# The MLP's first product as seven products of quarter operands, with weight sums partly by accumulating DMAs

## The chip, the cores and the metric
The kernel runs on one core of a Trainium2 chip. The metric is the time of one execution on the device in microseconds; the median of three runs is shown with the lowest and the highest.

## The reference
One layer of a diffusion backbone on 512 tokens of 1024 features, in float32. A token mixer of three branches (retention, Fourier, spatial gating) comes first; the part that matters here is the second sub-layer:

```
h2 = modulate(rms_norm(x, g_pre_mlp[l]), sh2, sc2)
x = x + gt2 * rms_norm(sq_relu_mlp(h2, w_up[l], w_down[l]), g_post_mlp[l])

def sq_relu_mlp(h, w_up, w_down):
    a = jax.nn.relu(h @ w_up)
    return (a * a) @ w_down
```
`w_up` is 1024 x 4096, `w_down` 4096 x 1024.

## The kernel before
Activations lie transposed, features on partitions and tokens on the free axis. Each float32 operand is written once in two parts of the type float32r, `hi` (the rounded part, written by ACT, L105 or L126) and `lo` (the exact rest, by DVE, L108 or L127). A product of 128 features by 128 features on some tokens is three instructions on PE, hi*hi, hi*lo and lo*hi, accumulated in PSUM (`mm3`, L131 to L133).

PE and SP (the queue of the weight loads) keep the order in which the program is written; the instructions of the other engines are ordered when the program is built, by priority and readiness, and each engine then runs its list in that order. Weights come in chunks of 128 x 1024 values (512 KB), in the order of `plan`: `fetch` loads one into `raw` (3 buffers, L102) and splits it into `whi` and `wlo` (3 buffers each). `chunk(kind, n, ahead)` hands one out and fetches the next ones. `slots` are 28 buffers of 4 KB a partition for long-lived tiles, `aux` 9 of the same size. `background` (L387) loads one row block of `w_mod` on POOL's queue into a tile `wmod2` (2 buffers), once PE's latest product is done, and runs the matvec of the one before on DVE (L240).

Before the MLP the output projection runs in two halves of 256 tokens (`out_proj`), and the norm of one half (`mix_residual`, then `mlp_input`) behind the products of the other. Both begin with `total` (L851), a sum over partitions by PE; the reciprocal root (`rstd`) and the rest are on DVE and ACT. `mlp_input` writes the MLP's input h2 in two parts, one feature tile at a time (L248, L252, L253). The first quarter of the hidden features (`up_first`, L935) is taken in the two halves of 256 tokens, for each row tile of `w_up` that meets an h2 tile; the three further quarters (`up`) are products of 512 tokens. `activate` takes relu and square on ACT and splits the hidden features. `down` follows a quarter behind and adds into y on DVE (L980); the last quarter's `down` runs in halves again (`last_down`, L1003), and `finish` adds the residual and stores. The order of the products around the first quarter is:

```
    up_first(0, 0)
    up_first(0, 1)
    mix_residual(1)
    for k in range(2, 7):
        up_first(0, k)
    mlp_input(1)
    up_first(0, 7)
    up_first_done(0)
```
Of the kernel before, what the change touches and what calls it, by code (L numbers as in the profile page):

```python
# [16 lines left out]
F32 = mybir.dt.float32  # L17
# [18 lines left out]
def kernel(ctx: ExitStack, tc: tile.TileContext, i: dict, out: bass.AP):  # L36
# [42 lines left out]
    plan += [("upr", k) for k in range(KT)] + [("up", KT + m) for m in range(KT)]  # L79
    for q in range(1, 4):  # L80
        plan += [("down", KT * (q - 1) + m) for m in range(KT)]
        plan += [("up", KT * (q + 1) + m) for m in range(KT)] if q < 3 else []
    plan += [("down", 24 + m) for m in range(KT)]
# [3 lines left out]
    place.update({("upr", k): aux if 2 <= k <= 5 else slot for k in range(KT)})  # L87
    place.update({("down", 24 + m): slot for m in range(6)})
    source = {"kq": "w_kq", "u": "w_u", "vs": "w_vs", "f": "w_f", "gate": "w_gate", "v": "w_v", "dft_l": "dft_l",
              "k": "w_k", "g": "w_g", "out": "w_out", "abc": "w_abc", "upr": "w_up0", "up": "w_up", "down": "w_down"}  # L90
# [4 lines left out]
    def fetch(later=False):  # L95
        """Load the next [128, 1024] weight chunk of the plan and split it into (hi, lo)."""
# [5 lines left out]
        nc.sync.dma_start(out=raw, in_=i[source[key[0]]][{"v": key[1] % 4, "up": key[1] - KT}.get(key[0], key[1])])  # L102
# [15 lines left out]
    def chunk(kind, n, ahead=2):  # L118
        """A chunk of weights in two parts; the next ones of the plan are on their way."""
# [9 lines left out]
    def mm3(ps, w, x, first, last):  # L129
        """ps += w.T @ x with w = (hi, lo), x = (hi, lo)."""  # L130
# [7 lines left out]
    def product(ps, w, xs_, sl=slice(None)):  # L138
        """ps = w.T @ x for a chunk w of 8 row tiles."""
        for k in range(KT):  # L140
            ks = slice(128 * k, 128 * k + 128)
            mm3(ps, (w[0][:, ks], w[1][:, ks]), hl(xs_[k], sl), k == 0, k == KT - 1)

# [30 lines left out]
    vecs = const.tile([P, 10, KT], F32, name="vecs")       # b_mod (6), g_pre_mix, g_post_mix, g_pre_mlp, g_post_mlp  # L174
# [10 lines left out]
    def keep_warm(n):  # L185
        """Products that nobody reads, so that the tensor engine's clock is up when the data are there."""
# [23 lines left out]
    def rstd(sums, n, size, r, between=None):  # L210
        """r = (sum / n + eps) ** -0.5: a table's estimate and one Newton step. The sums are in PSUM, side by side."""
# [923 lines left out]
```

## Time and profile before

| | us |
|---|---|
| median of 3 runs (lowest to highest) | 794.76 (794.74 to 796.51) |
| the profiled execution, first to last instruction (span) | 793.4 |
| PE busy in it | 779.8 |
| DVE busy | 496.0 |
| ACT busy | 388.7 |

The span is the profiled execution's own time between its first and last instruction; what a run has around it is seen from the difference to the median, 1.4 us. PE's busy time is the time in which at least one product is in its pipeline, so neighbouring products overlap in it: one product is busy for longer than the distance to the next. Idle time of an engine that nobody waits for costs nothing.

### The profile page before, as it was taken

How to read it: one execution, taken by the hardware profiler on the slowest of the kernel's cores; microseconds unless marked ns; L12 is line 12 of the kernel's file. 1: busy time of each engine (PE TensorE's matmuls, PEld its weight loads, DVE VectorE, ACT ScalarE, POOL GpSimd, SP SyncE). 2: the span in 40 equal slices, each digit the busy share in tenths (PEclk: the TensorE clock that was granted, in tenths of full speed). 3: DMA queues.
4: the chain of work that ended last, by engine and by line, in shares of the span. 5: the costliest groups of instructions: out<-in, count | busy, mean ns of one | idle time of the engine just before them, and what ended most of it. 6: DMA issues, size and time to landing. Idle time of an engine off the chain costs nothing.

```text
span 793.4 us, 10284 instructions
## 1 busy us (share of the span) xinstructions
PE 779.8 (98%) x4066; PEld 668.7 (84%) x4066; DVE 496.0 (63%) x731; ACT 388.7 (49%) x585; POOL 38.1 (5%) x73
## 2 busy tenths in 40 slices
PE   9999999999999999999999999999999999999994
PEld 6888888888888888888999998888888888888993
DVE  6999997688898576599369735631333333336255
ACT  6337557657997443332477455432353124524222
POOL 0061000000000111100000001000000000000001
PEclk9999999999999999999999999999999999999997
DMA  9954242643224487635124024623223223225011
GB/s 346 379 179 133 93 138 81 204 152 108 87 99 137 154 296 264 227 116 193 49 87 141 11 81 159 205 88 107 98 88 107 92 94 107 88 98 186 1 54 54
DMA packets 31680, 106.74 MB, mean 135 GB/s; under 512 B 3704, under 2 KB 5888, under 8 KB 31632
## 3 DMA queue, kind: packets, MB, share of 16 engines
q1 hardware_dynamic: 26944, 89.25, 32.9%
q0 software_dynamic: 4672, 16.82, 6.2%
q8 instruction: 32, 0.52, 0.3%
q14 instruction: 16, 0.13, 0.1%
q10 hardware_dynamic: 16, 0.01, 0.0%
HBM read 103.97 MB, written 2.10 MB: 134 GB/s over the span
## 4 chain that ended last, share of the span: by engine, by line
PE 97%; DVE 2%; ACT 0%; issue 0%; POOL 0%; DVEq 0%; ACTq 0%; POOLq 0%
PE ps L132 27%; PE ps L133 27%; PE ps L131 27%; PE pu L935 5%; PE kq L356 5%; PE warm L189 1%; DVE y L1021 1%; PE ps L201 1%; PE ssx L273 0%; PE ps L473 0%; PE ps L472 0%; PE ps L471 0%; PE ps L649 0%; DVE sg L548 0%; PE ps L851 0%; DVE wlo L108 0%
## 5 line engine op out<-in xcount | busy, mean ns | idle before, releaser
L105 ACT ACTIVATE whi<-raw 128x1024 fp32r<-128x1024 f32 (+1 forms) x119 | 124.2, 1045 | 234.2 <-PE ps L132 201.5
L108 DVE TENSOR_TENSOR wlo<-raw,whi 128x1024 fp32r<-128x1024 f32 (+1 forms) x119 | 143.3, 1204 | 121.0 <-ACT whi L105 120.9
L133 PE MATMUL ps<-h,wlo 128*128 128x512 f32 x448 | 174.4, 389 | 0.3 <-DVE wlo L108 0.3
L131 PE MATMUL ps<-h,whi 128*128 128x512 f32 x448 | 174.7, 390 | 0.0
L132 PE MATMUL ps<-h,whi 128*128 128x512 f32 x448 | 174.4, 389 | 0.0
L133 PEld LDWEIGHTS ps<-h,wlo 128*128 128x128 f32 x448 | 84.1, 188 | 18.4 <-DVE wlo L108 0.8
L131 PEld LDWEIGHTS ps<-h,whi 128*128 128x128 f32 x448 | 84.1, 188 | 17.5
L132 PEld LDWEIGHTS ps<-h,whi 128*128 128x128 f32 x448 | 84.1, 188 | 17.1
L131 PE MATMUL ps<-a,whi 128*128 128x512 f32 (+1 forms) x224 | 83.7, 374 | 0.0
L132 PE MATMUL ps<-a,whi 128*128 128x512 f32 (+1 forms) x224 | 83.7, 374 | 0.0
L133 PE MATMUL ps<-a,wlo 128*128 128x512 f32 (+1 forms) x224 | 83.7, 374 | 0.0
L240 DVE CUSTOM_DVE_ANT_0 wmod<-wmod,cb,vecs 128x1024 f32<-128x1024 f32 x32 | 41.0, 1282 | 24.7 <-DMA wmod<-in_w_modT 24.7
L131 PEld LDWEIGHTS ps<-a,whi 128*128 128x128 f32 x224 | 42.2, 188 | 7.5
L133 PEld LDWEIGHTS ps<-a,wlo 128*128 128x128 f32 x224 | 42.2, 188 | 7.5
L132 PEld LDWEIGHTS ps<-a,whi 128*128 128x128 f32 x224 | 42.2, 188 | 7.4
L935 PE MATMUL pu<-h,rhi 128*128 128x256 f32 x256 | 45.6, 285 | 0.3 <-ACT h L252 0.3
L127 DVE TENSOR_TENSOR a<-relu,a 128x512 fp32r<-128x512 f32 (+1 forms) x40 | 22.7, 584 | 27.5 <-ACT a L126 27.5
L935 PEld LDWEIGHTS pu<-h,rhi 128*128 128x128 f32 x256 | 39.2, 192 | 0.5 <-ACT h L252 0.5
L387 POOL DMA_DIRECT2D wmod<-in_w_modT x32 | 17.0, 531 | 433.1 <-PE ps L133 230.8
L980 DVE TENSOR_TENSOR y<-y,ps 128x512 f32<-128x512 f32 x16 | 11.0, 686 | 40.9 <-PE ps L133 40.9
L935 PE MATMUL pu<-h,rlo 128*128 128x256 f32 x128 | 33.9, 283 | 0.0
L108 DVE TENSOR_TENSOR rlo<-raw,rhi 128x1024 fp32r<-128x1024 f32 x19 | 22.9, 1221 | 9.9 <-ACT rhi L105 9.1
(292 smaller groups left out, 1436.3 us busy)
## 6 DMA issues: line engine op xcount, KB each, us to landing
wmod<-in_w_modT POOLq DMA_DIRECT2D x32, 512.0 KB, 3.5
raw<-in_w_up SPq DMA_DIRECT2D x32, 512.0 KB, 3.3
raw<-in_w_down SPq DMA_DIRECT2D x32, 512.0 KB, 3.3
raw<-in_w_gate SPq DMA_DIRECT2D x24, 512.0 KB, 4.3
wmod<-in_w_modT SPq DMA_DIRECT2D x16, 512.0 KB, 8.5
x<-in_xT SPq DMA_DIRECT2D x8, 512.0 KB, 6.5
raw<-in_w_kq SPq DMA_DIRECT2D x8, 512.0 KB, 6.9
raw<-in_w_v SPq DMA_DIRECT2D x8, 512.0 KB, 4.0
```

Of the source, the lines that this page charges most:

```text
L105: S.activation(out=hi, in_=raw, func=AF.Copy)
L108: rest = lambda: V.tensor_tensor(out=lo, in0=raw, in1=f32(hi), op=ALU.subtract)
L127: V.tensor_tensor(out=dst_lo, in0=src, in1=f32(dst_hi), op=ALU.subtract)
L131: PE.matmul(ps, w[0], x[0], start=first, stop=False)
L132: PE.matmul(ps, w[0], x[1], start=False, stop=False)
L133: latest[0] = PE.matmul(ps, w[1], x[0], start=False, stop=last)
L189: PE.matmul(ps, ones, ones.unsqueeze(1).broadcast_to([P, 4, P]), start=True, stop=True)
L240: return V.tensor_tensor_reduce(out=prod, in0=wt, in1=cvec, scale=1.0, scalar=bias_col, op0=ALU.mult, op1=ALU.add, accum_out=dst_col)
L356: PE.matmul(kq[n], w[sub % 2][:, 128 * n:128 * n + 128], hs[k][:, sub // 2], start=k == 0 and sub == 0, stop=False)
L387: load = nc.gpsimd.dma_start(out=t, in_=i["w_modT"][j, k])
L935: latest[0] = PE.matmul(ps, w[a][:, 128 * m:128 * m + 128], x[b], start=k == 0 and (a, b) == parts[0] and m % 2 == 0, stop=k == KT - 1 and ...
L980: V.tensor_tensor(out=yk(m), in0=yk(m), in1=ps, op=ALU.add)
```

## The change
The up product is cut into quarters in three directions: the features of h2 in a lower and an upper half (rows 1 and 2), the tokens in two halves (N1, N2), and each pair of hidden feature tiles in its two tiles. Such a product of 2 x 2 blocks takes eight products of blocks; the changed kernel takes seven, of sums of blocks, for each of 16 units of two hidden feature tiles (`seventh`: 4 row tiles x 3 instructions of 256 tokens). On the side of the activations seven operands of four feature tiles each are kept in two parts: B11, B21, B22 and the sums T1 to T4 (`in_parts`, `mlp_sums`). On the side of the weights a unit has four operands: a (tile 2u as it is), b (two sums), c (w2 with the sum of its halves in the lower half) and d (one sum). `unit_weights` loads both tiles into two `raw` buffers (r1, r2). Three accumulating DMAs on POOL's queue (256 KB each) add parts of the weights in HBM to r2, r1 and x, and one sum is a DVE addition (x, in a `wmod2` buffer); ACT and DVE split a, b, c and d. A unit's outputs are combined from two accumulators in PSUM into a raw tile t by ACT and DVE, relu and square are one DVE instruction on t, and `split_hidden` writes the two parts.

The first products of units 0 to 7 (with a, on the first half of the tokens) run while the second half's norms are computed (`early`); the other five products of these units follow, then the down products of the first quarter, and units 8 to 11 and 12 to 15 after the first and the second quarter's. The pools keep their sizes. The diff removes the comments of the file as well, which is left out here.

```diff
-    plan += [("upr", k) for k in range(KT)] + [("up", KT + m) for m in range(KT)]
+    plan += [("upa", u) for u in range(KT)] + [("down", m) for m in range(4 * KT)]
...
-    h2 = [slot([P, 2, L], F32R, "h2") for _ in range(KT)]
+    full, parts = {}, {}
+    def in_parts(name, src, where):
+        hi, lo = where([P, 4, HT], F32R, "bhi"), where([P, 4, HT], F32R, "blo")
+        S.activation(out=hi, in_=src, func=AF.Copy)
+        V.tensor_tensor(out=lo, in0=src, in1=f32(hi), op=ALU.subtract)
+        parts[name] = (hi, lo)
     def mlp_input(half):
         r = tmp("rx2", HT)
         rstd([total(sums[half][:, 1])], D, HT, r)
...
+        for j in range(2):
+            b = full[j, half] = slot([P, 4, HT], F32, "h2")
+            for m in range(4 * j, 4 * j + 4):
+                if m % 2 == 0:
+                    pair = work.tile([P, 2, HT], F32, name="xr2", tag="t")
+                xr = pair[:, m % 2]
+                scaled(xr, xk(m)[:, halves[half]], gs2[:, m:m + 1], r)
+                S.activation(out=b[:, m % 4], in_=xr, func=AF.Identity, bias=mod[:, 3, m:m + 1])
             if half == 0:
+                in_parts(("B11", "B21")[j], b, slot)
+    def mlp_sums():
+        b11, b12, b21, b22 = full[0, 0], full[0, 1], full[1, 0], full[1, 1]
+        n2 = slot([P, 4, HT], F32, "n2")
+        V.tensor_tensor(out=b11, in0=b11, in1=b12, op=ALU.subtract)
+        V.scalar_tensor_tensor(out=n2, in0=b11, scalar=-1.0, in1=b22, op0=ALU.mult, op1=ALU.subtract)
+        in_parts("T2", n2, aux)
+        V.tensor_tensor(out=b12, in0=b22, in1=b12, op=ALU.subtract)
+        in_parts("T3", b12, aux)
+        in_parts("T1", b11, aux)
+        V.scalar_tensor_tensor(out=b21, in0=n2, scalar=-1.0, in1=b21, op0=ALU.mult, op1=ALU.subtract)
+        in_parts("T4", b21, aux)
+        in_parts("B22", b22, slot)
+    raw_hidden, hidden = {}, {}
+    weights = {}
+    def unit_weights(u):
+        w1, w2 = i["w_up"][2 * u], i["w_up"][2 * u + 1]
+        lower, upper = slice(0, 512), slice(512, 1024)
+        r1 = raw_pool.tile([P, D], F32, name="r1", tag="raw")
+        nc.sync.dma_start(out=r1, in_=w1)
+        r2 = raw_pool.tile([P, D], F32, name="r2", tag="raw")
+        nc.sync.dma_start(out=r2, in_=w2)
+        yield
+        if (u, "a") not in weights:
+            a = hi_pool.tile([P, D], F32R, name="whi", tag="whi"), lo_pool.tile([P, D], F32R, name="wlo", tag="wlo")
+            with tc.high_priority(offset=30):
+                split(*a, r1)
+            weights[u, "a"] = a
+        nc.gpsimd.dma_start(out=r2[:, lower], in_=w2[:, upper], accum_op=ALU.add)
+        yield
+        x = raw_pool.tile([P, 512], F32, name="s2", tag="wmod2", bufs=2)
+        with tc.high_priority(offset=30):
+            V.tensor_tensor(out=x, in0=r2[:, lower], in1=r1[:, lower], op=ALU.add)
+        nc.gpsimd.dma_start(out=r1[:, lower], in_=w2[:, lower], accum_op=ALU.add)
+        yield
+        b = hi_pool.tile([P, D], F32R, name="whi", tag="whi"), lo_pool.tile([P, D], F32R, name="wlo", tag="wlo")
+        with tc.high_priority(offset=30):
+            split(b[0][:, lower], b[1][:, lower], x)
+            split(b[0][:, upper], b[1][:, upper], r1[:, lower])
+        weights[u, "b"] = b
+        nc.gpsimd.dma_start(out=x, in_=w1[:, upper], accum_op=ALU.add)
+        yield
+        c = hi_pool.tile([P, D], F32R, name="whi", tag="whi"), lo_pool.tile([P, D], F32R, name="wlo", tag="wlo")
+        with tc.high_priority(offset=30):
+            split(*c, r2)
+        weights[u, "c"] = c
+        yield
+        d = hi_pool.tile([P, D], F32R, name="whi", tag="whi"), lo_pool.tile([P, D], F32R, name="wlo", tag="wlo")
+        with tc.high_priority(offset=30):
+            split(d[0][:, lower], d[1][:, lower], x)
+        weights[u, "d"] = d
+        yield
+    steps_of = {}
+    def prepare(u, n):
+        if u is None:
+            return
+        if u not in steps_of:
+            steps_of[u] = [unit_weights(u), 0]
+        while steps_of[u][1] < n:
+            next(steps_of[u][0])
+            steps_of[u][1] += 1
+    def seventh(ps, u, w, upper, x, first=False):
+        hi, lo = weights[u, w]
+        for k in range(4):
+            ks = slice(512 * upper + 128 * k, 512 * upper + 128 * k + 128)
+            for n, (a, b) in enumerate(((hi, 0), (hi, 1), (lo, 0))):
+                latest[0] = PE.matmul(ps, a[:, ks], parts[x][b][:, k], start=first and k == 0 and n == 0,
+                                      stop=k == 3 and n == 2, skip_group_check=True)
+    chain = {}
+    urgent = dict(offset=100)
+    N1, N2 = halves
+    def unit_first(u):
+        if u not in chain:
+            chain[u] = bank("chain")[:, 0:HT]
+        t = raw_hidden[u] = slot([P, 2, L], F32, "ru")
+        seventh(chain[u], u, "a", 0, "B11", True)
+        with tc.high_priority(**urgent):
+            S.copy(out=t[:, 0, N1], in_=chain[u])
+        p2 = bank()[:, 0:HT]
+        seventh(p2, u, "a", 1, "B21", True)
+        with tc.high_priority(**urgent):
+            V.tensor_tensor(out=t[:, 0, N1], in0=t[:, 0, N1], in1=p2, op=ALU.add)
+    def unit_rest(u):
+        t, ch = raw_hidden[u], chain[u]
+        following = None if u in (7, 11, 15) else u + 1
+        side = bank()[:, 0:HT]
+        prepare(following, 1)
+        seventh(ch, u, "b", 0, "T2")
+        with tc.high_priority(**urgent):
+            S.activation(out=t[:, 1, N1], in_=ch, func=AF.Copy, scale=-1.0)
+        seventh(side, u, "b", 1, "T3", True)
+        with tc.high_priority(**urgent):
+            S.activation(out=t[:, 1, N2], in_=side, func=AF.Copy, scale=-1.0)
+        prepare(following, 3)
+        seventh(ch, u, "c", 0, "T1")
+        with tc.high_priority(**urgent):
+            V.tensor_tensor(out=t[:, 1, N2], in0=t[:, 1, N2], in1=ch, op=ALU.subtract)
+        seventh(side, u, "c", 1, "T4")
+        with tc.high_priority(**urgent):
+            V.tensor_tensor(out=t[:, 1, N1], in0=t[:, 1, N1], in1=side, op=ALU.subtract)
+        prepare(following, 5)
+        seventh(ch, u, "d", 0, "B22")
+        with tc.high_priority(**urgent):
+            S.copy(out=t[:, 0, N2], in_=ch)
+        prepare(following, 6)
+        V.scalar_tensor_tensor(out=t, in0=t, scalar=0.0, in1=t, op0=ALU.max, op1=ALU.mult)
+    def split_hidden(u):
+        t = raw_hidden.pop(u)
+        hi, lo = slot([P, 2, L], F32R, "ahi"), slot([P, 2, L], F32R, "alo")
+        split(hi, lo, t)
+        for e in range(2):
+            hidden[2 * u + e] = (hi[:, e], lo[:, e])
...
+    def early(pair):
+        ps = bank("chain")
+        for u in (2 * pair, 2 * pair + 1):
+            weights[u, "a"] = chunk("upa", u, min(2, 7 - u))
+            chain[u] = ps[:, halves[u % 2]]
+            t = raw_hidden[u] = slot([P, 2, L], F32, "ru")
+            seventh(chain[u], u, "a", 0, "B11", u % 2 == 0)
+        for u in (2 * pair, 2 * pair + 1):
+            p2 = bank()[:, 0:HT]
+            seventh(p2, u, "a", 1, "B21", True)
+            t = raw_hidden[u][:, 0, N1]
+            S.copy(out=t, in_=chain[u])
+            V.tensor_tensor(out=t, in0=t, in1=p2, op=ALU.add)
+    early(0)
     mix_residual(1)
-    for k in range(2, 7):
-        up_first(0, k)
+    early(1)
     mlp_input(1)
-    up_first(0, 7)
-    up_first_done(0)
-    for k in range(KT):
-        up_first(1, k)
-        with tc.issue_after(last_lo[0].ins):
-            prefetch("up", KT + min(k // 2, 2))
-    up_first_done(1)
+    early(2)
+    early(3)
+    mlp_sums()
+    prepare(0, 6)
+    for u in range(KT):
+        unit_rest(u)
+        if u < 4:
+            split_hidden(u)
+        background()
...
-        product(ps, chunk("down", KT * q + m), [hidden[KT * q + k] for k in range(KT)])
+        product(ps, chunk("down", KT * q + m, min(2, 7 - m)), [hidden[KT * q + k] for k in range(KT)])
         if q == 0:
             S.copy(out=yk(m), in_=ps)
         else:
             V.tensor_tensor(out=yk(m), in0=yk(m), in1=ps, op=ALU.add)
-    for m in range(KT):
-        up(1, m)
-        background()
     V.tensor_tensor(out=gg2, in0=mod[:, 5], in1=vecs[:, G_POST2], op=ALU.mult)
-    for q in range(1, 4):
+    for q in range(3):
         for m in range(KT):
-            down(q - 1, m)
-        if q < 3:
-            for m in range(KT):
-                up(q + 1, m)
+            down(q, m)
+            if q < 2 and m >= 4:
+                prepare(8 + 4 * q, m - 3)
+                if m == 7:
+                    prepare(8 + 4 * q, 6)
+        for u in range(4 * q + 4, 4 * q + 8):
+            split_hidden(u)
+            if q < 2:
+                unit_first(u + 4)
+                unit_rest(u + 4)
...
-        "w_up0": _rows(a["w_up"][0][:, :D], 1),
-        "w_up": _tiles(a["w_up"][0][:, D:]),
+        "w_up": _tiles(a["w_up"][0]),
```

## Rows read from the trace of the kernel before

**Rows 1.** First part of the page: busy time, share of the span, instructions.
```profile
PE 779.8 (98%) x4066; PEld 668.7 (84%) x4066; DVE 496.0 (63%) x731; ACT 388.7 (49%) x585; POOL 38.1 (5%) x73
```
**Rows 2.** Stages by windows: PE, PEld, DVE, ACT, POOL busy (instructions), granted clock, DMA share, GB/s.
```profile
4.00:8.00 4.00, 4.00 (x14) 1.98 (x14) 2.40 (x4) 2.63 (x4) 0.24 (x1) 1.00 1.02 376
...
425.30:472.80 47.50, 47.23 (x391) 46.92 (x390) 30.34 (x60) 24.74 (x61) 0.00 (x0) 1.00 0.17 57
472.80:516.00 43.20, 43.20 (x193) 35.78 (x192) 24.77 (x35) 24.86 (x46) 3.70 (x7) 1.00 0.52 169
...
560.00:733.70 173.70, 173.70 (x768) 143.85 (x768) 66.52 (x69) 68.38 (x87) 0.00 (x0) 1.00 0.31 106
```
**Rows 3.** What PE waited for in the whole run: us in total, times, longest.
```profile
PE warm L189 <- POOL eps_h L167: 1.0, 1, 1.0
...
PE pu L935 <- ACT h L252: 0.3, 1, 0.3
```
**Rows 4.** The chain that ended last, in order of time: start, us, what.
```profile
425.48 5.76 PE pu L935 x48
431.24 0.43 PE ps L851 x2
431.67 14.39 PE pu L935 x120
446.06 0.45 PE ps L851 x2
```
**Rows 5.** Timelines of PE, DVE and ACT around the norms of both halves: start, us, instruction.
```profile
423.01 1.28 DVE L248 SCALAR_TENSOR_TENSOR xr<-x,gs,rx 128x256 f32<-128x256 f32 x3
...
425.31 0.88 PE L935 MATMUL pu<-h,rhi 128*128 128x256 f32 x6
...
434.81 2.36 DVE L887 TENSOR_TENSOR y<-y,ry 128x1024 f32<-128x1024 f32 x2
...
437.08 2.49 DVE L888 TENSOR_TENSOR x<-x,y 128x512 f32<-128x512 f32 x4
...
442.25 0.43 DVE L850 TENSOR_TENSOR sums<-sums 128x256 f32<-128x256 f32 x1
...
448.54 1.28 DVE L248 SCALAR_TENSOR_TENSOR xr<-x,gs,rx 128x256 f32<-128x256 f32 x3
...
453.81 0.91 ACT L252 ACTIVATE h<-xr,mod 128x256 fp32r<-128x256 f32 x2 [0.53 <-DVE xr L248]
```
**Rows 6.** Instructions of four tiles: ns min/median/max, first and last start.
```profile
L105 ACT ACTIVATE whi<-raw x119: 627/1061/1067, 14.3 to 732.5; 128x1024 fp32r<-128x1024 f32 x115, 128x516 fp32r<-128x516 f32 x4
L108 DVE TENSOR_TENSOR wlo<-raw,whi x119: 678/1225/1227, 16.3 to 733.5; 128x1024 fp32r<-128x1024 f32 x115, 128x516 fp32r<-128x516 f32 x4
...
L873 ACT ACTIVATE y<-ps x16: 363/383/385, 381.5 to 425.9; 128x256 f32<-128x256 f32 x16
...
L1003 DVE TENSOR_TENSOR y<-y,ps x16: 414/421/422, 737.0 to 780.6; 128x256 f32<-128x256 f32 x16
...
L240 DVE CUSTOM_DVE_ANT_0 wmod<-wmod,cb,vecs x32: 1272/1284/1289, 186.9 to 514.9; 128x1024 f32<-128x1024 f32 x32
```
**Rows 7.** Waits of SP's and POOL's queues from 380 us on: total, times, longest.
```profile
SPq L102 <- DVE wlo L108: 257.2, 48, 20.1
...
POOL wmod L387 <- PE ps L133: 29.5, 6, 4.9
```
**Rows 8.** DMA issues: KB each, median us to landing.
```profile
wmod<-in_w_modT POOLq DMA_DIRECT2D x32, 512.0 KB, 3.5
raw<-in_w_up SPq DMA_DIRECT2D x32, 512.0 KB, 3.3
...
raw<-in_w_gate SPq DMA_DIRECT2D x24, 512.0 KB, 4.3
wmod<-in_w_modT SPq DMA_DIRECT2D x16, 512.0 KB, 8.5
...
out_y<-x SPq DMA_DIRECT2D x8, 256.0 KB, 2.2
```
**Rows 9.** Landing times of the tile raw.
```profile
DMA to landing us min/median/max: 2.6/3.6/10.9
```
**Rows 10.** The end of the run by windows, columns as in rows 2.
```profile
782.00:784.00 2.00, 0.22 (x2) 0.00 (x0) 1.10 (x3) 0.90 (x3) 0.00 (x0) 1.00 0.00 0
784.00:786.00 2.00, 0.00 (x0) 0.00 (x0) 1.97 (x4) 0.00 (x0) 0.96 (x1) 0.83 0.00 0
786.00:788.00 2.00, 0.00 (x0) 0.00 (x0) 2.00 (x3) 0.00 (x0) 1.32 (x2) 0.50 0.21 74
```

More of the change, by code (lines that the diff above doesn't have):

```diff
@@ L86 @@
     place[("out", 7)] = slot
-    place.update({("upr", k): aux if 2 <= k <= 5 else slot for k in range(KT)})
     place.update({("down", 24 + m): slot for m in range(6)})
     source = {"kq": "w_kq", "u": "w_u", "vs": "w_vs", "f": "w_f", "gate": "w_gate", "v": "w_v", "dft_l": "dft_l",
-              "k": "w_k", "g": "w_g", "out": "w_out", "abc": "w_abc", "upr": "w_up0", "up": "w_up", "down": "w_down"}
+              "k": "w_k", "g": "w_g", "out": "w_out", "abc": "w_abc", "upa": "w_up", "down": "w_down"}
     ready = {}
@@ L101, in fetch @@
         raw = raw_pool.tile([P, size], F32, name="raw", tag="raw")
-        nc.sync.dma_start(out=raw, in_=i[source[key[0]]][{"v": key[1] % 4, "up": key[1] - KT}.get(key[0], key[1])])
+        nc.sync.dma_start(out=raw, in_=i[source[key[0]]][{"v": key[1] % 4, "upa": 2 * key[1]}.get(key[0], key[1])])
         hi = where([P, 1024], F32R, "rhi") if where else hi_pool.tile([P, size], F32R, name="whi", tag="whi")
@@ L141, in product @@
             ks = slice(128 * k, 128 * k + 128)
-            mm3(ps, (w[0][:, ks], w[1][:, ks]), hl(xs_[k], sl), k == 0, k == KT - 1)
+            x = xs_[k]
+            x = (x[0][:, sl], x[1][:, sl]) if isinstance(x, tuple) else hl(x, sl)
+            mm3(ps, (w[0][:, ks], w[1][:, ks]), x, k == 0, k == KT - 1)
     xs, wmod1 = [], []
@@ L893, in mlp_input @@
         rstd([total(sums[half][:, 1])], D, HT, r)
-        for m in range(KT):
-            if m % 2 == 0:
-                pair = work.tile([P, 2, HT], F32, name="xr2", tag="t")
-            xr = pair[:, m % 2]
-            scaled(xr, xk(m)[:, halves[half]], gs2[:, m:m + 1], r)
-            last_lo[0] = shifted(h2[m][:, 0, halves[half]], h2[m][:, 1, halves[half]], xr, mod[:, 3, m:m + 1])()
-    hidden = {}
-    def activate(n, sl, ps):
-        r = tmp("relu", sl.stop - sl.start)
-        S.activation(out=r, in_=ps, func=AF.Relu)
-        S.activation(out=r, in_=r, func=AF.Square)
-        split(hidden[n][:, 0, sl], hidden[n][:, 1, sl], r)
@@ L911, in up @@
-    def up(q, m):
-        n = KT * q + m
-        w = chunk("up", n)
-        hidden[n] = (aux if q % 2 else slot)([P, 2, L], F32R, "a2")
-        ps = bank()
-        product(ps, w, h2)
-        activate(n, slice(0, L), ps)
-    last_lo = [None]
-    wu = []
-    pus = {}
-    def up_first(half, k):
-        if half == 0:
-            wu.append(chunk("upr", k, min(3, 7 - k)))
-        if k == 0:
-            pus[half] = [bank("pu") for _ in range(4)]
-        w = wu[k]
-        x = hl(h2[k], halves[half])
-        parts = ((0, 0), (1, 0), (0, 1))
-        for m, (a, b) in ([(m, p) for p in parts for m in range(KT)] if k == 0 else
-                          [(m, p) for m in range(KT) for p in parts]):
-            ps = pus[half][m // 2][:, HT * (m % 2):HT * (m % 2) + HT]
-            latest[0] = PE.matmul(ps, w[a][:, 128 * m:128 * m + 128], x[b],
-                                  start=k == 0 and (a, b) == parts[0] and m % 2 == 0,
-                                  stop=k == KT - 1 and (a, b) == parts[2], skip_group_check=True)
@@ L939, in up_first_done @@
-    def up_first_done(half):
-        for m in range(KT):
-            if half == 0:
-                hidden[m] = slot([P, 2, L], F32R, "a2")
-            activate(m, halves[half], pus[half][m // 2][:, HT * (m % 2):HT * (m % 2) + HT])
+        for j in range(2):
[6 more added lines that the diff above has]
+                S.activation(out=b[:, m % 4], in_=xr, func=AF.Identity, bias=mod[:, 3, m:m + 1])
+            if half == 0:
+                in_parts(("B11", "B21")[j], b, slot)
@@ L950 @@
         out_proj(1, m)
-        prefetch("upr", min(m, 4))
     mlp_input(0)
@@ L980, in down @@
             V.tensor_tensor(out=yk(m), in0=yk(m), in1=ps, op=ALU.add)
-    for m in range(KT):
-        up(1, m)
-        background()
     V.tensor_tensor(out=gg2, in0=mod[:, 5], in1=vecs[:, G_POST2], op=ALU.mult)
-    for q in range(1, 4):
+    for q in range(3):
         for m in range(KT):
-            down(q - 1, m)
-        if q < 3:
-            for m in range(KT):
-                up(q + 1, m)
+            down(q, m)
[8 more added lines that the diff above has]
+                unit_rest(u + 4)
     wd = {}
```

5 lines of the change are left out of this document (removed).

## The prediction
> **What bounds the kernel now.** I read the page's first part, the stages by windows, the waits, the chain of waits around the start of the MLP, the DMA issues. The reader is to see that PE is busy 98% of the span at the full clock [rows 1], and in the MLP without a gap, while DVE is busy 30.3 of 47.5 us in the first quarter of the up product and 24.8 of 43.2 in the second, and ACT about as much or less [rows 2]. PE's longest wait on anything in the whole run is 1.0 us, and 0.3 in front of any product of the MLP [rows 3]. So the kernel's time is its list of products, and the change is worth what it takes off that list, less every gap that it opens, because today there are none.
>
> What a product costs is its distance to the next one, not its busy time: 48 products of 256 columns take 5.76 us and 120 take 14.39 [rows 4], 0.120 each; 768 of 512 columns take 173.7 [rows 2], 0.226 each. Two of 256 cost 0.240, 6% more than one of 512.
>
> **The change part by part.**
>
> *Products.* Before: the first quarter in 384 products of 256 (46.1 us), three quarters in 576 of 512 (130.3): 176.4 us. After: 16 units of 7 x 12 products, 1344 of 256 columns: 161.3. Minus 15.1 us; one eighth fewer columns would be 22, but the narrow ones give a third back. The down products keep number and shape.
>
> *Operands of the first half later: +2.0 (0 to 2.5).* Before, PE needs only one feature tile of h2 to begin, and waited 0.3 us for it [rows 3]. After, B11 wants four tiles, then a split over 1024 elements: `scaled` four times at 0.40 (three in 1.28 less overlap), an Identity 0.45 [rows 5], hi 1.06, lo 1.22 [rows 6]: 4.3 us from the norm's factor, which is there at 423.0. Before, the first product starts 2.3 us after that point, at 425.3 [rows 5].
>
> *Less cover between two norms: +5.2 (4.5 to 5.7).* PE's queue has the two sums over partitions (`total`) of the second half in order. Before, 120 products lie between them, 14.4 us [rows 4]. The work they cover runs from the first, 431.24, to the last sum on DVE, 442.25 + 0.43 [rows 5]: 11.4 us. After, only early(1) stands there, 48 products, 5.76 us, and the second `total` blocks PE, since early(2) and early(3) are queued behind it. 11.4 - 0.4 - 5.8 = 5.2.
>
> *The seven sums' operands: +5 (0 to 11).* From the second `total` to T2: the root 2.5 us (446.06 to 448.54), eight `scaled` 3.2, an Identity 0.5, two sums at 1.18 (two of 1024 in 2.36), hi 1.06, lo 1.2 [rows 5, 6]: 10.8; early(2) and (3) cover 96 x 0.12 = 11.5. But the same DVE has in that time a chunk's lo, the first unit's sum and splits, four additions: 4.8 more. 0 to 4 late; I take 2. T1, T3, T4 and B22 are six more DVE instructions of 1.18, 7.1 us, beside a first unit whose PE time is 60 x 0.12 = 7.2 and which has its own 7.6 of DVE (next paragraph). 0 to 7; I take 3.
>
> *The early eight units: +19.6 (3 to 34, and 104 in the worst case).* Each has 7.2 us of products. DVE's part per unit, at 0.62 for 512 elements, 1.18 for 1024, 0.42 for 256 (grouped rows [rows 5]): x 0.62, b 1.24, c 1.18, d 0.62, two evacuations 0.84, relu squared 1.18; a hidden split 1.18 in four of eight and one w_mod row 1.28 [rows 6] in all: 7.6 on average. DVE alone would be the bound, by 0.4 us a unit plus what is left of the operands above. The longer chain is in the buffers. `raw` has three, and a unit holds two (r1, r2) until its splits are done, so r2 of unit u+1 can't be loaded before a buffer of unit u is free; SP waits for just this today (DVE's lo, 257 us in 48 waits [rows 7]), at no cost because a chunk then lasts 5.4 us of PE. From there: load 3.3, accumulating DMA into r2, and then either the split of r2 (1.06 + 1.22) frees the buffer, or the sum x 0.62, the second accumulating DMA into r1, and the split of half of it (0.62 + 0.62). No row has an accumulating DMA. From below 2.2 (a 256 KB store), from above 8.5 (512 KB where all queues were full at 376 GB/s [rows 2]); I take 3.5, the loads on POOL's queue, whose path it shares [rows 8]. The short loop is 3.3 + 3.5 + 2.3 = 9.1, the long one 3.3 + 3.5 + 0.6 + 3.5 + 1.2 = 12.1. Which closes first is a matter of how ACT's and DVE's queues are written, which no row shows; r2's data are there 4.1 us earlier, so I take 9.1 and 0.9 for queueing behind a DVE that is busy three quarters of it: 10.0, so 2.8 us of PE idle at each of seven handovers. Low end: DVE's bound, 7 x 0.4; high end: the long loop, 7 x 4.9, or with two accumulations of 8.5 a loop of 22.1, 7 x 14.9. Waits also move to POOL: its queue holds the three accumulations and the w_mod load, which waits for a unit's last product; POOL waits for PE up to 4.9 us at a time today [rows 7], and an accumulation behind it would wait as long. I take nothing for it.
> [...]
>
> *The later eight: +4 (0 to 12).* 84 products, 10.1 us, against 9.1 or 12.1; six handovers, units 8 and 12 being prepared behind the down products, where DVE is idle (66.5 of 173.7 us busy [rows 2]). I take 0.7 each.
>
> *What hides.* Evacuations between the products of one accumulator: 12 others lie between, 1.44 us, against 0.38 to 0.42 [rows 6] and at worst an ACT split of 1.06 ahead: nothing (up to 0.2 each). 16.8 MB more traffic: under 250 GB/s in the densest stretch, where loads took 4.3 instead of 3.3 [rows 8]; that is in the 0.9. ACT: 5 of 7.2 us.
>
> **Sum.** -15.1 + 2.0 + 5.2 + 5 + 19.6 + 4 = +20.7 on a span of 793.4: 814.1. The median of the runs is 1.4 above the span: 815.
>
> **The rivals.**
> 1. *The list of products decides (faster).* The order of ACT and DVE lets r2 go early, the w_mod rows slip behind, and only the gap of 5.2 and the 2.0 remain: 794.8 - 15.1 + 7.2 = 787. For it: PE has hardly waited for anything so far [rows 3]. Against it: that was with splits of 2.3 us in 5.4; now DVE has more than 100%. Chance 0.11.
> 2. *DVE is the bound, not the DMAs.* The early eight cost 7.1 + 8 x 0.4 = 10, the later none: 794.8 - 15.1 + 7.2 + 2 + 10 = 799. For it: the quickest load of a chunk landed in 2.6 us [rows 9]. Chance 0.13; a hand's breadth better on one term gives no change, 0.07.
> 3. *The long loop (slower still).* r1 is freed first: 7 x 4.9 + 6 x 2.0 = 46.3 in place of 23.6: 838. It decides as soon as an accumulation takes over 4 us or b's split stands before c's. Chance 0.18.
> 4. *The clock.* [...] Chance 0.09. [...]
>
> **How the numbers follow.** The forecast has 0.42. Range 786 to 850: left out are half of rival 1 and most of rival 4; an accumulation of 8.5 us would be far outside and has no load to match it. What a measurement here can tell from no change is 0.3%, 792.4 to 797.1. Faster 0.11 (rival 1), same 0.07, slower 0.82.
>
> **What would show it.** The gap in PE before the second `total` of about 5 us; in each of units 1 to 7 a wait of PE's weight load for the lo of b (DVE), that for a DMA from w_up, and SP waiting for DVE; DVE near 80% in that stretch; products at 0.120. Wrong, if PE runs the 16 units without gaps of over a microsecond, or if the early stretch from `early(0)` to the first down product lasts less than 23 + 58 + 10 us.

## The result: 878 us in place of 795, and the profile after

The changed kernel took 877.87 us (median of four, 877.73 to 881.06), the kernel before 794.95: a ratio of 1.105 (95% interval 1.103 to 1.107). The forecast was 815, its range 786 to 850: the sign held, the size did not. The profiled execution is the slowest of the four, span 879.3; some 2 us of that lie ahead of the MLP (the last product of the output projection starts at 426.65, in most of the runs below at 424.5 to 424.9).

The first part of the page of after, against [rows 1]:
```profile
PE 800.3 (91%) x4450; PEld 699.5 (80%) x4450; DVE 575.8 (65%) x830; ACT 403.1 (46%) x600; POOL 78.5 (9%) x121
```
PE has more busy time although it has 15 us fewer products at full clock, and 79 us idle where it had 14. The stages by windows (columns as in [rows 2]): early groups, units 0 to 7, first down stage, units 8 to 11, second down stage, units 12 to 15:
```profile
428.60:467.40 38.80, 27.69 (x196) 26.64 (x196) 30.38 (x48) 22.98 (x42) 2.64 (x3) 0.87 0.41 105
467.40:581.30 113.90, 77.70 (x480) 70.79 (x481) 66.55 (x88) 36.47 (x61) 22.12 (x28) 0.84 0.61 157
581.30:624.90 43.60, 43.60 (x194) 36.13 (x194) 13.02 (x12) 13.24 (x19) 2.60 (x3) 1.00 0.41 109
624.90:679.80 54.90, 46.24 (x338) 44.69 (x337) 30.58 (x41) 24.24 (x39) 7.84 (x9) 0.91 0.52 128
679.80:723.30 43.50, 43.50 (x194) 36.02 (x193) 17.43 (x19) 8.99 (x11) 2.62 (x3) 1.00 0.38 109
723.30:776.00 52.70, 45.34 (x337) 43.72 (x336) 33.25 (x44) 25.61 (x40) 7.89 (x9) 0.94 0.53 125
```
At 0.120 us a product, the four stages of the up product would take 23.0, 57.6, 40.3 and 40.3 us. They take 38.8, 113.9, 54.9 and 52.7. The down stages, with DVE and ACT mostly idle (busy 13.0 and 13.2 of 43.6 us in the first), are as they were (43.6 and 43.5 us, for 44.0 before, from 516 to 560 us). No engine is full in units 0 to 7 (PE 77.7 and DVE 66.6 of 113.9), so a chain of waits is the place to look. PE's waits from the last output projection to unit 0, and then the longest in units 0 to 7:
```profile
PE ps L849 <- DVE sums L848: 7.3, 1, 7.3
...
PE chain L990 <- ACT bhi L894: 3.1, 2, 1.6
...
PE ps L990 <- ACT whi L122: 10.2, 7, 3.3
PE chain L990 <- ACT ru L1031: 6.5, 4, 2.8
PE chain L990 <- ACT whi L122: 5.8, 3, 2.8
PE chain L990 <- DVE blo L895: 4.8, 1, 4.8
```
The rows name ACT and DVE, but these wait in turn. The chain of waits from 500 to 517 us follows a unit's splits back (start, us, what):
```profile
499.80 5.57 DMA r<-in_w_up
...
505.43 0.48 issue
...
505.93 3.73 DMA r<-in_w_up
...
509.74 0.70 DVE s L951
...
510.53 0.64 ACT whi L122
...
511.19 0.69 DVE wlo L123
511.88 1.14 DVE ru L1033
513.01 1.15 DVE wlo L123
...
514.18 5.52 DMA r<-in_w_up
```
This is one turn, 14.38 us; PE starts the units 14.4 us apart in the mean (unit 0 at 467.4, unit 7 at 568.3). r2 is loaded (5.57), the first accumulating DMA is issued and lands (0.56 and 3.73), and then c's split, which frees r2 for the next load, is not the next thing on DVE: the sum x, the lo of b's lower half and the squared relu of the unit before stand ahead of it (it ends 4.5 us after the landing). The DMA issues from 467 to 580 us (KB each, median us to landing):
```profile
r<-in_w_up SPq DMA_DIRECT2D x12, 512.0 KB, 5.2
r<-in_w_up POOLq DMA_DIRECT2D x14, 256.0 KB, 3.7
wmod<-in_w_modT POOLq DMA_DIRECT2D x7, 512.0 KB, 6.0
...
s<-in_w_up POOLq DMA_DIRECT2D x7, 256.0 KB, 6.3
```

### The profile page after: what moved, and what is told of

The parts are those of the page before. It is cut to its first block, busy times and chain, and to the rows that moved or that the text cites. A ratio compares the mean times of both kernels' runs of the same rounds, so it can differ in the third digit from the quotient of the medians.

```text
span 879.3 us, 11423 instructions
## 1 busy us (share of the span) xinstructions
PE 800.3 (91%) x4450; PEld 699.5 (80%) x4450; DVE 575.8 (65%) x830; ACT 403.1 (46%) x600; POOL 78.5 (9%) x121
## 3 DMA queue, kind: packets, MB, share of 16 engines
q0 software_dynamic: 11584, 29.41, 14.8%
## 4 chain that ended last, share of the span: by engine, by line
PE 65%; DMA 16%; DVE 9%; issue 6%; ACT 3%; POOL 0%; POOLq 0%; SPq 0%; DVEq 0%; ACTq 0%
PE ps L128 17%; PE ps L127 17%; PE ps L129 17%; DMA r<-in_w_up 12%; PE kq L354 4%; PE chain L990 4%; DMA s<-in_w_up 3%; DVE wlo L123 3%; PE ps L990 2%; ACT whi L122 1%; DVE wlo L104 1%; DMA raw<-in_w_down 1%; DMA x<-in_xT 1%; DVE ru L1033 1%; DVE s L951 1%
## 5 line engine op out<-in xcount | busy, mean ns | idle before, releaser
L990 PE MATMUL chain<-bhi,whi 128*128 128x256 f32 x256 | 82.3, 321 | 31.2 <-DVE ru L1024 8.3
L129 PE MATMUL ps<-h,wlo 128*128 128x512 f32 x256 | 99.7, 390 | 0.3 <-DVE wlo L104 0.3
L127 PE MATMUL ps<-h,whi 128*128 128x512 f32 x256 | 100.0, 391 | 0.0
L128 PE MATMUL ps<-h,whi 128*128 128x512 f32 x256 | 99.7, 390 | 0.0
L990 PE MATMUL chain<-blo,whi 128*128 128x256 f32 x256 | 79.7, 311 | 7.1 <-DVE blo L895 7.1
L127 PE MATMUL ps<-ahi,whi 128*128 128x512 f32 (+1 forms) x224 | 83.8, 374 | 0.0
L128 PE MATMUL ps<-alo,whi 128*128 128x512 f32 (+1 forms) x224 | 83.8, 374 | 0.0
L129 PE MATMUL ps<-ahi,wlo 128*128 128x512 f32 (+1 forms) x224 | 83.7, 374 | 0.0
L990 PE MATMUL chain<-bhi,wlo 128*128 128x256 f32 x256 | 79.9, 312 | 0.7 <-DVE wlo L123 0.7
L990 PE MATMUL ps<-bhi,whi 128*128 128x256 f32 x192 | 58.4, 304 | 15.7 <-ACT whi L122 12.2
L122 ACT ACTIVATE whi<-s 128x512 fp32r<-128x512 f32 x32 | 20.2, 631 | 86.9 <-DVE s L951 41.1
L128 PEld LDWEIGHTS ps<-h,whi 128*128 128x128 f32 x256 | 48.0, 188 | 9.9
L127 PEld LDWEIGHTS ps<-h,whi 128*128 128x128 f32 x256 | 48.1, 188 | 9.9
```

Of the source, the lines that this page charges most:

```text
L122: S.activation(out=dst_hi, in_=src, func=AF.Copy)
L127: PE.matmul(ps, w[0], x[0], start=first, stop=False)
L128: PE.matmul(ps, w[0], x[1], start=False, stop=False)
L129: latest[0] = PE.matmul(ps, w[1], x[0], start=False, stop=last)
L990: latest[0] = PE.matmul(ps, a[:, ks], parts[x][b][:, k], start=first and k == 0 and n == 0, stop=k == 3 and n == 2, skip_group_check=True)
```

## The experiments

The kernel before ran beside each batch at 794.6 to 795.3 us. e9 and e10 are medians of five executions, the others one execution each; those of after lie 3.3 us apart, so a difference of that size between two runs decides nothing. A stage runs from its first product to the next stage's; the first row has the products alone, at 0.120 us each.

```
run                     us      early  units 0-7  8-11  12-15   edit
(products alone)                23.0     57.6     40.3  40.3
after                  877.9    38.8    113.9     54.9  52.7
e1_no_acc              820.3    40.4     79.8     40.8  40.7   three sums left out
e2_plain_dma           844.9    38.1     99.3     42.1  43.8   plain copies in their place
e3_bg_later            865.4    38.7    103.6     53.2  50.9   w_mod work moved
e4_r2_slots            870.4    46.1    101.0     52.1  52.5   more raw buffers
e5_pool_sums           849.6    41.3     95.4     45.4  46.5   sums on GpSimd
e6_dve_sums            819.9    40.4     79.0     41.0  40.8   sums on DVE
e7_order13             874.5    40.5    108.8     55.9  50.4   other order at the start
e8_warm                886.0    40.0    123.7     52.4  50.5   more products
e9_sums_dve_bg         812.8    39.4     72.4     41.0  40.8   e6, e3 and e7 together
e10_second_half_only   790.4                      41.1  40.8   sevenths for units 8-15 alone
e11_no_T               868.6    36.9    110.4     53.6  48.8   T1 to T4 left out
e12_first_link_dve     853.1    39.4    101.6     45.0  47.0   first sum on DVE
```

**1. Without the accumulating DMAs (e1_no_acc).**
```diff
-        nc.gpsimd.dma_start(out=r2[:, lower], in_=w2[:, upper], accum_op=ALU.add)
...
-        nc.gpsimd.dma_start(out=r1[:, lower], in_=w2[:, lower], accum_op=ALU.add)
...
-        nc.gpsimd.dma_start(out=x, in_=w1[:, upper], accum_op=ALU.add)
```


> The three accumulating DMAs of each unit are left out (the sums are then incomplete; everything else, all waits on DVE and ACT included, stands). Theory A, the buffer loop: an early unit's period of 14.3 us is load of r2 (5.6 with its company on the queues) - accumulation 3.7 - the split of r2 behind x, b and relu squared (4.4) - next load. Without the accumulations the loop is about 4 + 4.4 = 8.4, so seven handovers shrink by 5.9 each and the later eight units (27 us over their products now) lose their waits: 877.9 - 41 - 22 = 815. Theory B, the engines: DVE, ACT and the half clock set the period, not the transfers: over 850.


820.25: 57.6 us of the 83 go. The later eight units come down to their products (40.8 and 40.7 for 40.3), units 0 to 7 lose 34 of their 56, the start keeps its loss. Some 22 us stay in units 0 to 7 without any accumulation; experiment 9 comes back to them.

**2. Plain copies (e2_plain_dma).** `accum_op=ALU.add` is dropped in the three lines; queue, bytes and waits stay.

> The same three DMAs as plain copies over the same bytes on the same queue (the sums are then wrong). Theory A: what costs is a further hop through the DMA queues in series with the load, not the addition in it: 878 within 6. Rival: the read and the write back of the destination make the transfer slow; then each hop is over 1 us shorter and the time at least 20 us lower, under 858.


844.89, the rival's region: 33 us hang on the adding itself. But 25 hang on there being a transfer at all, as theory A had it. The issues of e2 in units 0 to 7:
```profile
r<-in_w_up SPq DMA_DIRECT2D x12, 512.0 KB, 4.3
...
r<-in_w_up POOLq DMA_DIRECT2D x13, 256.0 KB, 3.0
```
The loads on the other queue land earlier too, 4.3 us for 5.2. The accumulations can't be the whole reason: in e1, which has none, the same loads took 5.5 (first row, from 467 to 547 us), and in after from 624 to 776 us, with accumulations and without the w_mod loads, 3.5 (second row).
```profile
r<-in_w_up SPq DMA_DIRECT2D x11, 512.0 KB, 5.5
```
```profile
r<-in_w_up SPq DMA_DIRECT2D x12, 512.0 KB, 3.5
```
So something else counts too; that it is what runs beside a load (the w_mod load, the next unit's r1) is the author's reading, and the shares were not taken apart. What the accumulating transfers asked of the DMA engines shows in the queue rows (packets, MB, share of 16 engines) from 624 to 776 us, where only these transfers use POOL's queue; first after, then e2:
```profile
q0 software_dynamic: 3152, 5.74, 23.6%
```
```profile
q0 software_dynamic: 1440, 4.72, 9.1%
```
For each MB the accumulating ones had 549 packets and 4.1% of the engines' time, the plain ones 305 and 1.9%: about double.

**3. The w_mod work moved (e3_bg_later).** `background()` is called after each `down(0, m)` instead of after each early unit; the small DVE product `gg2` moves behind the down products with it.

> The last eight w_mod loads and their DVE instructions move from the early units to the first quarter's down products. Theory A: the 512 KB load no longer stands ahead of the third accumulation on POOL's queue nor beside r2's load, which goes from 5.6 to about 4.1; the loop from 14.3 to 12.7: 877.9 - 11 = 867. Rival, DVE is the bound of the early units: 1.3 us of DVE less in each, also about 10 us, but then r2's load to its accumulation stays at 6.1. Rival, neither: 878.


865.41, near theory A's number: units 0 to 7 lose 10. In the turn that begins at 521 us r2's load takes 4.64 us, and units 0 to 7 are shorter by 1.3 us each.

**4. More raw buffers (e4_r2_slots).**
```diff
-        r2 = raw_pool.tile([P, D], F32, name="r2", tag="raw")
+        r2 = slot([P, D], F32, "r2") if u < KT else raw_pool.tile([P, D], F32, name="r2", tag="raw")
```


> r2 of the early eight units goes into the long-lived 4 KB buffers, of which some are free then, so that raw's three serve r1 alone and the next unit's load and first accumulation need not wait for a split. Theory A: the load and the first hop leave the loop; what is left is x, its third accumulation and d's split around the two wmod2 buffers, or DVE, about 10 us: 877.9 - 7 x 4.3 = 848, the later eight unchanged. Rival, the chain of accumulations within a unit sets the period, whatever the buffers: 870 or more.


870.35, the rival's number. Units 0 to 7 lose 13 us, 7 of which come back at the start. With the loop through r2 opened, the next one closes; POOL's waits in those units:
```profile
POOL r L952 <- DVE s L951: 41.2, 8, 16.0
POOL wmod L385 <- PE chain L990: 27.6, 6, 11.4
```
The second accumulation waits for x, which stands on DVE behind other work, up to 16 us; the w_mod load ahead of a third accumulation waits for PE. So r2's buffer is one of several chains; how long each of the others is was not measured.

**5 and 6. The same sums on an engine.** In both, the adds run in the places of the three transfers (r1's lower half first, then x, r2's lower half, and x again); G in e5, V in e6:
```diff
-        nc.gpsimd.dma_start(out=r2[:, lower], in_=w2[:, upper], accum_op=ALU.add)
+        with tc.high_priority(offset=30):
+            V.tensor_tensor(out=r1[:, lower], in0=r1[:, lower], in1=r2[:, lower], op=ALU.add)
...
-            V.tensor_tensor(out=x, in0=r2[:, lower], in1=r1[:, lower], op=ALU.add)
-        nc.gpsimd.dma_start(out=r1[:, lower], in_=w2[:, lower], accum_op=ALU.add)
+            V.tensor_tensor(out=x, in0=r2[:, upper], in1=r1[:, lower], op=ALU.add)
+            V.tensor_tensor(out=r2[:, lower], in0=r2[:, lower], in1=r2[:, upper], op=ALU.add)
...
-        nc.gpsimd.dma_start(out=x, in_=w1[:, upper], accum_op=ALU.add)
+        with tc.high_priority(offset=30):
+            V.tensor_tensor(out=x, in0=x, in1=r1[:, upper], op=ALU.add)
```


> The same sums in the same places, but each added inside the memory of the core by GpSimd (it reads r2's two halves, which the two plain loads have brought), and no accumulating DMA. GpSimd's one tensor operation of 128x512 in the trace took 1.58 us. Theory A (the price of the sums is the way of an accumulating DMA: issue, landing and the wait behind it, 5 to 6 us a link): the later eight units come to 41 us for each four as they do without the sums, units 0 to 7 to 80-92, total 820-833. Rival (it is the order itself, one sum after the other before the splits, wherever they are made): units 0 to 7 above 95, each later four above 43, total 843 or more.

> The same sums on VectorE, three more of 128x512 at 0.69 us for each unit, 2.1 us. Theory A (links through DMA are the price, DVE has room at 65% busy): units 0 to 7 at 80-86, later fours 41-42, total 820-827. Rival (what is left in units 0 to 7 without accumulations, 22 us, is DVE's own queue: splits, squares, hidden splits, matvecs in order): each unit grows by the 2.1 us, units 0 to 7 at 95-100, total 836-842.


On DVE: 819.94, as quick as leaving the sums out, theory A in each stage (its ranges begin 1 us above what units 0 to 7 took). So the sums cost nothing to speak of; their way through the DMAs cost 58 us. On GpSimd 849.62, the rival's region. There an add took 1.3 to 2.1 us (from 500 to 530 us), and DVE's own instructions took longer than in e6. The lo of a split in the trace of e5, 467 to 545 us (min/median/max ns), and then in e6:
```profile
L123 DVE TENSOR_TENSOR wlo<-s,whi x12: 677/692/1746, 472.5 to 543.0; 128x512 fp32r<-128x512 f32 x12
```
```profile
L123 DVE TENSOR_TENSOR wlo<-s,whi x15: 672/682/691, 467.4 to 541.7; 128x512 fp32r<-128x512 f32 x15
```
In e5 the mean of the twelve was 993 ns and the longest 1746, though half of them took 692 or less; in e6, where GpSimd adds nothing, the mean was 680 and the longest 691.

**7. Both early groups ahead of the second half's input (e7_order13).**
```diff
     early(1)
+    early(2)
     mlp_input(1)
-    early(2)
     early(3)
```


> Only the order of the start is changed: the two groups of early products (u 2-3 and 4-5) that stood on both sides of the second half's MLP input now both stand ahead of it, 6.2 us more of products between the two waits on DVE sums. Theory A (cover: the 7.3 us wait for the second sum of squares is only short of work beside it): that wait falls to about 1, the wait ahead of T2, which has less in front of it, grows by 3 to 6; total 873-878. Rival (the wait is work queued on DVE and not the chain to the sum, so it moves along): the two waits together stay 12 us or more and the total is 878 or above.


874.5 lies in theory A's range, but no further from after than two executions of one kernel lie apart. The waits from the last output projection through unit 0:
```profile
PE chain L990 <- ACT bhi L894: 8.7, 2, 7.0
PE chain L990 <- DVE blo L895: 3.1, 2, 2.3
PE ps L849 <- DVE sums L848: 2.4, 1, 2.4
```
The wait for the sum falls from 7.3 to 2.4; the one for T2 rises, from 1.6 for its hi and 5.1 for its lo to 7.2 and 1.2. Together they fall from 14.0 to 10.8: the first not to 1, as theory A had it, and the second grows by 1.7 and not by 3 to 6. The chain on DVE and ACT stays; the order of PE's work decides in the main where it shows.

**8. More products (e8_warm).** After each group of a unit, eight products into the other half of `side`'s bank. The hidden features of those units are others in this run.
```diff
+        if spare is not None:
+            for n in range(8):
+                latest[0] = PE.matmul(spare, parts["T2"][0][:, n % 4, 0:128], parts["T2"][0][:, n % 4], ...)
```


> After each of the five groups of a unit (units 0 to 7 only) TensorE runs eight more products of 256 columns into an unused half of a bank, which nothing reads; 8 x 0.120 = 0.96 us, 4.8 us a unit against about 7 us that TensorE waits there. Theory A (the loop of loads, sums and splits sets the period of 14.3 us, the half clock is its effect): the granted clock of units 0 to 7 goes to full, their sum stays 112-116, total 875-880. Rival (the half clock is a part of the loss: 125 products at 0.2135 in place of 0.120, 11.7 us): units 0 to 7 at 100-104, total 864-868. Third, the added products stand in the way (products that are ready wait up to 0.96 us): units 0 to 7 at 118 or more.


885.98. The window of units 0 to 7, without the last eight added products:
```profile
467.30:589.50 122.20, 104.58 (x792) 102.17 (x792) 65.36 (x88) 37.31 (x61) 22.12 (x28) 0.93 0.60 148
```
The granted clock is 0.93 for 0.84: if all that is missing of 1.00 is time at half clock (granted 0.50), that is 17 of 122 us for 36 of 114, an estimate from the two means. Yet the stage takes 8 us more: the third case. The added products stood in the way themselves, so the run shows that a higher clock bought in this way gains nothing, and not what the half clock costs; that the waits come first is seen from e1 and e6.

**9. What the runs point to, with sevenths (the seven products of sums) throughout (e9_sums_dve_bg).** The edits of e6, e3 and e7 together.

> Sevenths throughout, with what the runs so far point to: the sums on VectorE, the w_mod loads and their matvecs moved behind units 0 to 7 (one with each product of the first quarter's down projection), and the early groups u 2-3 and u 4-5 both ahead of the second half's MLP input. With the sums on VectorE alone DVE was busy for 95% of 482 to 546 us. Theory A (DVE is what then bounds units 0 to 7; 16 matvecs of 1.28 us, 20 us, leave it): units 0 to 7 at 64-70, total 802-810. Rival (the raw buffers and their loads bound them): units 0 to 7 stay above 75, total 813-818. In neither case below the kernel before, since the start's 14 to 17 us stay.


812.75, a ratio of 1.022 (1.021 to 1.024), between the two: units 0 to 7 come to 72.4, neither under 70 nor over 75. DVE's share in e6, then in e9:
```profile
467.00:546.00 79.00, 65.89 (x479) 62.56 (x480) 73.94 (x109) 37.26 (x61) 3.69 (x7) 0.94 0.43 147
```
```profile
467.00:543.00 76.00, 66.99 (x493) 63.23 (x494) 68.34 (x94) 38.45 (x63) 0.00 (x0) 0.95 0.33 108
```
DVE is busy 73.9 of 79.0 us in e6 and 68.3 of 76.0 in e9 (3.6 us of neighbouring stages in it). With the transfers gone it is the engine that fills units 0 to 7 most, but what of the 14.8 us above the products is DVE and what is the load's way was not taken apart further.

**10. Sevenths for units 8 to 15 alone (e10_second_half_only).** Units 0 to 7 and the start are the kernel before's; T1 to T4 are made from h2's two parts beside the first four down products, the weight sums on DVE.
```diff
+    for m in range(KT):
+        up(m)
+        background()
+    operands()
...
             down(q, m)
+            if q == 0 and m < 4:
+                mlp_sums(m)
```


> Sevenths for units 8 to 15 alone, with the sums on VectorE; units 0 to 7 and the start of the MLP are the kernel before's eight products, and T1 to T4 are made from h2's two parts beside the first four products of the down projection (four times 2 operations of 512, 4 of 256 and four splits). Theory A (all that the change lost was in the start, in units 0 to 7 and in the accumulating DMAs; units 8 to 11 and 12 to 15 then take 41 us each in place of the 44.1 that eight products take): 2 x 3 us gained, total 787-791 against 794.6. Rival (the operands' work, 4 to 5 us of DVE for each of four down products, or the later splits of four units' hidden features push products back): the first down stage grows from 43.6 by 3 us or more and the total is 793 or above.


790.36, a ratio of 0.994 (0.993 to 0.996): the only version that beats the kernel before, by 4.5 us. The first down stage, units 8 to 11 and units 12 to 15:
```profile
515.50:560.20 44.70, 44.70 (x199) 37.03 (x198) 15.12 (x17) 13.97 (x19) 0.00 (x0) 1.00 0.27 91
560.20:601.30 41.10, 41.10 (x338) 40.59 (x337) 34.04 (x49) 23.59 (x39) 0.00 (x0) 1.00 0.30 101
644.80:685.60 40.80, 40.80 (x338) 40.45 (x337) 36.80 (x52) 25.96 (x40) 0.00 (x0) 1.00 0.28 91
```
PE has no gap, and 15.1 of 44.7 us of DVE hide the operands' making. A quarter by eight products takes 192 x 0.226 = 43.4 us [rows 2], not the 44.1 of the expectation; by sevenths 41.1 and 40.8. That is 4.9 us for both.

**11. Without T1 to T4 (e11_no_T).** The seven operations and four splits go; the units use B11 and B21 in their place.

> The seven operations that make T1 to T4 and their four splits are left out; the units use B11 and B21 in their place, so the hidden features are others. Theory A (the start is held by one chain on DVE and ACT from the last output projection through two norms to the operands, 40 us beside 23 us of early products; the operands are its last part): the wait ahead of unit 0 (6.9 us in all) falls under 2, the early stage from 38.8 to 32-35, total 870-873. Rival (the wait ahead of unit 0 is for the first unit's weights, b's splits behind accumulations): early stage within 1 us of 38.8, total 876-879.


868.59, less than theory A said, but not as it said. The waits through unit 0 in this run:
```profile
...
PE chain L983 <- DVE ru L1017: 3.9, 1, 3.9
PE chain L983 <- DVE blo L895: 2.3, 1, 2.3
PE chain L983 <- ACT ru L1024: 1.8, 1, 1.8
...
```
The two waits for T2 (6.7 us) are gone (the 2.3 is B11's); new ones of 3.9 for DVE and 1.8 for ACT stand in unit 0. DVE's timeline shows where the first comes from:
```profile
472.44 0.69 DVE L944 TENSOR_TENSOR s<-r,r 128x512 f32<-128x512 f32 x1 [5.63 <-DMA r<-in_w_up]
473.05 0.41 DVE L1017 TENSOR_TENSOR ru<-ru,chain 128x256 f32<-128x256 f32 x1
```
DVE sat idle for 5.6 us, until unit 1's first accumulation had landed and its sum x could run, and the evacuation (an accumulator's way out of PSUM) that PE needed stood behind that sum in DVE's list. The early stage fell by 1.9 us only; the 32 to 35 had counted the wait for T2's lo in it, which lies in unit 0. Units 0 to 7 fell by 3.5 us and the later eight by 5.2, though DVE has the same instructions there (41 and 43 for 41 and 44); why was not taken apart.

**12. Only the first sum on DVE (e12_first_link_dve).**
```diff
-        nc.gpsimd.dma_start(out=r2[:, lower], in_=w2[:, upper], accum_op=ALU.add)
+        with tc.high_priority(offset=30):
+            V.tensor_tensor(out=r2[:, lower], in0=r2[:, lower], in1=r2[:, upper], op=ALU.add)
```


> Only the first of the three sums (r2's lower half plus its upper half) is made on VectorE, 0.69 us; the other two stay accumulating DMAs. Theory A (the loop goes through r2: load 5.6, first accumulation 0.5 + 3.7, c's split 4.5 later; the first sum is its only DMA link beside the load): the period falls by about 3.5 us to 10.5-11.5, units 0 to 7 at 85-95, total 845-857. Rival (each of the three links stands in its own way, the second one, 5.4 us ahead of b's upper half, as much): units 0 to 7 fall by a third of what all three cost (34), to 100-105, total 860-868.


853.06, theory A's total by the rival's stages: units 0 to 7 at 101.6 lose 12.3, a third of 34, where the loop through r2 alone would have given 19 or more; but the later eight lose 15.6 of the 26 that all three links cost. In them r2's way counts for more than half, in units 0 to 7 for no more than its share.

## Why the forecast was short by 63 us

By stages, against the products, in the profiled executions:

```
                 forecast   measured
start               9.2       17.7    (426.65 to 467.4 less 23.0)
units 0 to 7       22.6       56.3    (19.6, and 3 for the late T1, T3, T4)
units 8 to 15       4         27.0
products          -15.1      -15.1
sum                20.7       85.9
```
**The products** were right: 1344 at 0.120, and in e1, e6, e9 and e10 the later units run at that.

**The early eight units: this step failed, by 34 us.** It put the loop at "3.3 + 3.5 + 2.3 = 9.1" with 0.9 for queueing. The loop was the right one of the two, and three of its terms were too small: the load 5.6 for 3.3, the issue and the accumulation 4.3 for 3.5, and the split with what stands ahead of it 4.5 for 3.2: 14.4 for 10.0. The load's price came from stages in which fewer other transfers run (DMA share 0.17 to 0.52 [rows 2]); here (0.61) a w_mod load, the next unit's r1 and the accumulations run beside it (4.64 without the w_mod load in one turn of e3, 5.5 without accumulations in e1). The bounds held the accumulation (2.2 to 8.5), and the high end of this term, 34, was some 20 short, since the long loop too was made with the undisturbed load and without queueing. DVE, which was to be near 80% busy there, was busy 58%: the sign that the loop was longer than thought. e2's plain transfers took 3.0 and 4.5 us (medians of the two destinations, r and x), the accumulating ones 3.7 and 6.3. The range fell with this step: its upper end left out an accumulation of 8.5 us, which did not come, and had no room for a load, an accumulation and a split that are all longer at once.

**The later eight: failed, by 23.** "0.7 each" for six handovers assumed a loop shorter than a unit's 10.1 us of products. With transfers of 3.7 and 5.0 us there it is longer than that too, and e1 and e6 put all of it down to them: 26 of 27 us go.

**The start: short by 8.5.** Less cover cost 7.3 for 5.2, B11's operand 4.4 for 2.0, T2's hi 1.6 (its lo 5.1 more, in unit 0; 2 and 3 were put down for both and the later sums), and 23 products ran at half clock, 2.1 us; the two products of the norms, 0.9, are in the 17.7 as well, and 1.4 are spread. The waits come through DVE's and ACT's lists, where the splits of early chunks and of unit 0 stand among the norm's steps; e7 and e11 move them more than they remove them. T2's lo is an example (the second row); on DVE it stands behind the lo of unit 0's d, and that one's hi waits for an accumulation on ACT (the first row):
```profile
469.73 0.63 ACT L122 ACTIVATE whi<-s 128x512 fp32r<-128x512 f32 x1 [2.38 <-DMA s<-in_w_up]
```
```profile
471.33 1.22 DVE L895 TENSOR_TENSOR blo<-n,bhi 128x1024 fp32r<-128x1024 f32 x1
```

**What hides: put at nothing, and wrong.** An evacuation's own cost, 0.38 to 0.42, was right, and ACT's 5 of 7.2 us too (36.5 us in eight units). But the prediction let an evacuation wait for an ACT split of 1.06 at worst. PE's longest waits for evacuations from 380 us on:
```profile
PE chain L990 <- DVE ru L1024: 8.3, 4, 3.1
...
PE chain L990 <- ACT ru L1031: 6.5, 4, 2.8
PE chain L990 <- ACT ru L1017: 6.5, 4, 3.5
```
With two smaller rows they come to 25.7 us, to 12.6 in e1 and to 1.3 in e6. They are a part of the losses above and not a further one: ACT and DVE keep the order of their lists, and an evacuation stands behind a split or a sum that waits for a transfer, as in e11.

**The rivals.** DVE as the bound (799) is what e9 comes near, 812.8 with the larger loss at the start. The long loop (838) is right in that more than r2's way counts (e12), at a price too small. The clock did fall between products, to the 0.50 of [rows 10], and over 200 of the 1344 products ran at half clock (granted 0.50); but the fall followed the waits. Without the transfers (e1) the granted clock was 0.94 for 0.84 in units 0 to 7 and 1.00 for 0.91 and 0.94 in the later eight, and e8 raised it without gain.

## What to carry to other kernels

When a change puts a loop through buffers, price each link in the state that the change makes: the transfers beside all that will run with them (a 512 KB load of w_up landed after 3.3 us in the kernel before and 5.5 in units 0 to 7 of e1, medians), and the instruction that frees the buffer with what stands ahead of it on its engine. An instruction that waits for a transfer holds up everything behind it in its engine's list, the evacuations too (in e11 DVE sat idle for 5.6 us ahead of a sum, and PE waited 3.9 for the evacuation behind it). If a transfer only adds two things of which the core holds both, try the add on an engine with room: here it took 0.69 us on DVE, and the transfer 0.87 to issue and 3.7 to 6.3 to land (medians). Fewer products pay where PE has no other wait: the same sevenths cost 18 us throughout, at their best, and won 4.5 where the operands could be made beside other work.

## What the hardware showed that was not expected

- An accumulating DMA of 256 KB took POOL's queue 0.87 us to issue (mean of the 16 of L947), the plain copy in its place 0.54, and its transfer had 1.8 times the packets and 2.1 times the engines' time of a plain one for each byte (549 for 305 packets, 4.1% for 1.9%, a MB). Issues from 380 to 800 us, of after and then of e2:
```profile
L947 POOL DMA_DIRECT2D r<-in_w_up x16 | 14.0, 872 | 275.5 <-DVE w L218 117.9 <-DMA r<-in_w_up 72.9 <-DVE y L1092 36.5
```
```profile
L947 POOL DMA_DIRECT2D r<-in_w_up x16 | 8.6, 537 | 252.9 <-DVE w L218 117.9 <-DMA r<-in_w_up 65.4 <-DVE y L1092 36.0
```
- At half clock (granted 0.50) a product of 256 columns followed the last after 0.2135 us, not 0.240, twice the 0.120 of full clock. The window after the wait of 2.3 us at the start, and two products in a row in it:
```profile
431.70:433.20 1.50, 1.50 (x9) 1.50 (x9) 0.49 (x1) 0.97 (x1) 0.00 (x0) 0.50 0.29 117
```
```profile
431.86 0.41 PE L990 MATMUL chain<-bhi,whi 128*128 128x256 f32 x1
432.07 0.41 PE L990 MATMUL chain<-blo,whi 128*128 128x256 f32 x1
```
